# Splitting the second layer's mixer weights during the first FFN up projection of a two-layer DiT block

## The chip, the cores and the metric

The kernel runs on one core of a Trainium2 chip. The metric is the time of one execution on the device in microseconds; a kernel's figure is the median of several executions.

## The reference

The reference computes two layers of a diffusion transformer block on 512 latent tokens and 256 context tokens of width 1024, all in float32. Each layer modulates the normalized tokens, sends them through four parallel mixers (gated linear attention, pooling, a spatial gating unit, a 31-wide convolution module), projects back, normalizes, and applies a convolutional FFN with a hidden width of 2816. In the last layer the context only feeds the linear attention's state.

```python
for l in range(DEPTH):                      # DEPTH = 2
    with_ctx_out = l < DEPTH - 1
    h_lat = modulate(x, m_lat[0], m_lat[1]); h_ctx = modulate(ctx, m_ctx[0], m_ctx[1])
    y_lat, y_ctx = token_mixer(h_lat, h_ctx, w_in[l], ..., with_ctx_out)
    x = layer_norm(ALPHA * x + m_lat[2] * y_lat, ...)
    f_lat = conv_ffn(modulate(x, m_lat[3], m_lat[4]), ffn_w_up[l], ffn_conv_w[l], ffn_w_down[l], ...)
    x = layer_norm(ALPHA * x + m_lat[5] * f_lat, ...)
    if with_ctx_out:
        ...                                 # the same for ctx
```

`token_mixer` multiplies the tokens by `w_in`, whose columns are the mixers' inputs; `conv_ffn` multiplies by `w_up`, convolves 3x3 over rows of 64 tokens, gates with silu and multiplies by `w_down`.

## The kernel before

Every large product is made of three matmuls, to keep float32 accuracy with operands of fewer bits. An operand is split into a high part (a copy to the type fp32r, here *hi*) and a low part (the operand minus its high part, *lo*); `mm3` accumulates hi by hi, hi by lo and lo by hi in one PSUM bank. Activations are split once a stage (tiles hl, ll for latent tokens, hc, lc for context tokens). Weights are split as they arrive: `load_w` loads a 128x1024 tile into a stage buffer `st` (three of them, `wst`), ScalarE copies it to `hi` (L147; four buffers, `whi`), and GpSimd subtracts in two halves into `lo` (L133; four buffers, `wlo`). In some places VectorE subtracts instead.

The stages follow each other in the order of the program: mixers of layer 0 (to about 265 us), output projection, FFN up projection (to about 731 us), FFN down projection (to about 938 us), then the same for layer 1, whose mixers run from about 938 to 1097 us. The stages overlap at their edges. The order on each engine's queue is set when the program is built, by the tile framework's scheduler, and every engine takes its queue in order. All loads and stores are issued from SyncE's queue (SP).

The mixers of layer 1 (`mixers(1)`, `full` false) take 18 weight tiles of `w_in`: ten feature tiles (`w_feat`, 128 columns each, first four of them in `feat_halves`, then `feat`), four of `w_tokA` (128x576) and four of `w_tokB` (128x1024) in `tok`. The token projection A needs the context columns hc, lc too, which come out of the layer norm of the last down group by way of `to_hT` (L333 to L344). From its result come the decay logits (`lg`, L546), g (L549 to L553), the cumulative sums (`cum`, L568), the decayed keys (L599), the chunk states (`kv`, L620) and the attention itself (L649 to L691). The convolution's 31 taps for two channel tiles (L703) run on VectorE in the meantime.

The first up projection (`ffn_up(0, ...)`) loops over 44 weight tiles. For each, 24 matmuls of 512 columns and 24 of 256 run on TensorE, and ScalarE and VectorE apply nine convolution taps from PSUM (L889, L891, L918); a pair of tiles is gated by ScalarE and GpSimd (L921, L922) into gT. After the load of each tile, `fill(2)` takes two units from `queue`. Before the change these are 48 units of the second layer's modulation: 32 dots on VectorE (`dot_units`, L292) and 16 row products on TensorE (`row_units`, L251). Both load into one ring of three 128x1024 buffers (tag `ms`).

Of the kernel before, what the change touches and what calls it, by code (L numbers as in the profile page):

```python
# [58 lines left out]
def kernel(  # L59
# [72 lines left out]
    def sub_lo(eng, lo, src, hi):  # L132
        eng.tensor_tensor(out=lo, in0=src, in1=f(hi), op=ALU.subtract)  # L133
# [9 lines left out]
    def load_w(src, n, lo_eng=None, st=None):  # L143
        st = st or load_st(src, n)
        hi = whi.tile([128, 1024], F32R, tag="hi", name="hi")
        lo = wlo.tile([128, 1024], F32R, tag="lo", name="lo")
        S.activation(out=hi[:, :n], in_=st[:, :n], func=AF.Copy)  # L147
        if lo_eng is V:
            sub_lo(V, lo[:, :n], st[:, :n], hi[:, :n])
        else:  # L150
            for a, b in ((0, n // 2), (n // 2, n)):
                sub_lo(G, lo[:, a:b], st[:, a:b], hi[:, a:b])
        return hi, lo

    def mm3(ps, wh, wl, xh, xl, first, last, w_stationary=True):
# [268 lines left out]
    def mixers(l, ms=None, pre=()):  # L424
# [21 lines left out]

        def feat_halves(ids):

            ws = [load_w(w_feat[l, i], D) for i in ids]
            ps = [bank(f"fl{i}") for i in ids]  # L450
            for c0, c1 in ((0, 256), (256, 512)):
                for (hi, lo), pl in zip(ws, ps):
                    for k in range(KT):
                        w = slice(k * 128, (k + 1) * 128)
                        mm3(pl[:, c0:c1], hi[:, w], lo[:, w], hl[k][:, c0:c1], ll[k][:, c0:c1], k == 0, k == KT - 1)
            return [(pl, None) for pl in ps]

        def feat(i, ctx_too):
            hi, lo = load_w(w_feat[l, i], D)
            fill(3)  # L460
            pl = bank(f"fl{i}")
            pc = bank(f"fc{i}") if ctx_too else None
            for k in range(KT):
                w = slice(k * 128, (k + 1) * 128)
                mm3(pl, hi[:, w], lo[:, w], hl[k], ll[k], k == 0, k == KT - 1)
            if ctx_too:
                for k in range(KT):
                    w = slice(k * 128, (k + 1) * 128)
                    mm3(pc[:, :CTX], hi[:, w], lo[:, w], hc[k], lc[k], k == 0, k == KT - 1)
            return pl, pc  # L470
# [3 lines left out]
            if pc is not None:  # L474
                S.activation(out=dst[:, coff:coff + CTX], in_=pc[:, :CTX], func=func, **kw)

        def tok(src, n, passes, lo_eng=None, pre=()):
            ps, ws = {}, []
            for pi, (tiles, pool) in enumerate(passes):
                for t in tiles:  # L480
                    ps[t] = bank(f"tk{t}", pool[t])
                for k2 in range(KT // 2):
                    if pi == 0:
                        ws.append(load_w(src[l, k2], 2 * n, lo_eng, pre[k2] if k2 < len(pre) else None))
                        fill(3)
                    hi, lo = ws[k2]
                    for kk in range(2):
                        k = 2 * k2 + kk
                        s = slice(kk * n, (kk + 1) * n)
                        for t in tiles:  # L490
                            xh, xl = hcol(k, t)
                            mm3(ps[t][:, :n], hi[:, s], lo[:, s], xh, xl, k == 0, k == KT - 1, False)
            return ps
# [25 lines left out]
            conv_in()  # L519


        pa = tok(w_tokA, 288, [(range(NT), {t: "big" if t < 4 else "sm" for t in range(NT)})], V if full else G, pre)
        if full:
            with tc.issue_after(behind[0]):
                nc.sync.dma_start(out=cvw, in_=convw)
# [212 lines left out]

        lat_p = (range(4), {t: "big" for t in range(4)})
        ctx_p = (range(4, 6), {t: "big" for t in range(4, 6)})  # L740
        pb = tok(w_tokB, 512, [ctx_p, lat_p] if full else [lat_p])
        r_ = mx.tile([128, NT, 256], F32, name="r")
        vg = mx.tile([128, NT, 256], F32, name="vg")
        for t0, n in spans:
# [360 lines left out]
    for l in range(DEPTH):  # L1105
# [4 lines left out]
            out_proj(l, [(0, 1), (4, 5), (2,), (3,)], {0: (2, 3), 1: (4, 5), 4: (6, 7), 5: (2, 3), 2: (4, 5), 3: (6, 7)})  # L1110
        else:
            out_proj(l, [(0, 1), (2,), (3,)], [(1, 4), (2, 3), (0, 5), (1, 4)])
        with tc.tile_pool(name=f"gT{l}", bufs=1, side="right") as gp, \
                tc.tile_pool(name=f"gs{l}", bufs=3, side="right") as gs:
            gT = [gp.tile([128, TOK if l == 0 else LAT], F32, name=f"gT{i}") for i in range(NF)]
            with ExitStack() as es:
                conv = es.enter_context(tc.tile_pool(name=f"conv{l}", bufs=2))
                if l + 1 < DEPTH:
                    ms = es.enter_context(tc.tile_pool(name="msB", bufs=3))
                    rows, dots = row_units(l + 1, 0, ms), dot_units(l + 1, ms)  # L1120
                    for i in range(8):
                        queue.extend(dots[4 * i:4 * i + 4] + rows[2 * i:2 * i + 2])
                if l == 0:
                    rings(sm=[0, 1], big=[2, 3, 4, 5, 6], md=[7])
                else:
                    rings(big=[2, 3, 0, 5, 1, 4])
                ffn_up(l, gT, conv)
            if l == 0:
                ffn_down(l, gT, gs, [(0, 1, 2, 3), (4, 5)], {0: (0, 1), 1: (2, 3), 2: (4, 5), 3: (6, 7), 4: (0, 1), 5: (2, 3)})
            else:  # L1130
                ffn_down_last(l, gT, [(0, 1), (5, 4), (6, 2), (7, 3)])
# [130 lines left out]
```

## Time and profile before

| what | us |
| --- | --- |
| median of 3 runs | 1527.33 (1527.18 to 1527.73) |
| the profiled execution | 1527.78 |
| its span, first to last instruction | 1526.0 |
| TensorE matmuls busy | 1450.8 (95%) |
| VectorE busy | 1191.2 (78%) |
| GpSimd busy | 844.5 (55%) |
| ScalarE busy | 546.3 (36%) |

The granted TensorE clock is 0.98 of 2.4 GHz in the mean. The DMA engines moved 193 MB, 126 GB/s over the span. The busy shares are means over stages that differ; a busy TensorE counts a matmul from its start to its modelled end, so the table says which engine to look at and not where time can be won. Profiles name a line of the program as L133 and a tile by its name in the program; a weight split on GpSimd is `POOL lo L133`, its copy on ScalarE `ACT hi L147`.

### The profile page before, as it was taken

The page shows a single profiled execution, that of the slowest core. Times are in us where ns is not written, and L with a number is a line of the kernel's source. Part 1 is how long each engine was busy: PE and PEld are TensorE (multiplying, and loading weights), DVE is VectorE, ACT ScalarE, POOL GpSimd, SP SyncE. Part 2 cuts the span into 40 slices and gives each one's busy share as a digit, 9 for nine tenths or more (in the row PEclk, how much of TensorE's full clock was granted, in tenths as well). Part 3 has the DMA queues.
Part 4 walks back from the last instruction along what each step waited for, and adds up shares of the span by engine and source line. Part 5 has one row for each costly group of instructions (what it writes and reads, how often), then busy time and mean ns, then how long its engine had stood idle before and what let it go on. Part 6 is the DMA issues. An engine that isn't in the chain of part 4 may idle for free.

```text
span 1526.0 us, 22207 instructions
## 1 busy us (share of the span) xinstructions
PE 1450.8 (95%) x8389; PEld 1187.7 (78%) x8389; DVE 1191.2 (78%) x1896; ACT 546.3 (36%) x936; POOL 844.5 (55%) x695
## 2 busy tenths in 40 slices
PE   6999899998899999999999989989999999999997
PEld 5776567788688888888888768865678888888875
DVE  6429987796998877777432898798777999889596
ACT  5443224244223233233211235354426444443121
POOL 2433534454444444343444698646555888777374
PEclk9999899999999999999999999999999999999998
DMA  9545310635755521212433364221172323232531
GB/s 375 193 163 178 118 50 15 234 125 185 256 171 174 174 64 56 70 58 67 165 97 97 121 221 145 90 68 43 31 249 75 113 88 107 94 99 85 179 110 56
DMA packets 56827, 193.03 MB, mean 126 GB/s; under 512 B 6136, under 2 KB 6792, under 8 KB 55696
## 3 DMA queue, kind: packets, MB, share of 16 engines
q1 hardware_dynamic: 56720, 191.61, 37.4%
q8 instruction: 66, 1.08, 0.3%
q14 instruction: 41, 0.34, 0.1%
HBM read 181.08 MB, written 10.51 MB: 126 GB/s over the span
## 4 chain that ended last, share of the span: by engine, by line
PE 69%; DVE 13%; POOL 6%; DMA 5%; issue 4%; ACT 3%; SPq 0%; POOLq 0%; DVEq 0%; ACTq 0%
PE ul L157 10%; PE ul L158 10%; PE ul L159 10%; PE f L161 5%; PE f L162 5%; PE f L163 5%; POOL lo L133 3%; DVE acc L703 3%; PE uc L157 2%; PE uc L159 2%; PE uc L158 2%; PE fl L157 2%; DMA st<-in_w_up 2%; PE fl L159 1%; PE fl L158 1%
## 5 line engine op out<-in xcount | busy, mean ns | idle before, releaser
L133 POOL TENSOR_TENSOR lo<-st,hi 128x512 fp32r<-128x512 f32 (+1 forms) x336 | 469.6, 1421 | 342.9 <-ACT hi L147 298.4
L918 DVE SCALAR_TENSOR_TENSOR acc<-ul,cvw,acc 128x441 f32<-128x441 f32 (+2 forms) x660 | 437.9, 689 | 59.6 <-ACT acc L889 36.5
L147 ACT ACTIVATE hi<-st 128x1024 fp32r<-128x1024 f32 (+1 forms) x194 | 202.1, 1044 | 438.3 <-PE f L163 164.6
L158 PE MATMUL ul<-ll,hi 128*128 128x512 f32 (+1 forms) x768 | 286.1, 374 | 0.3 <-DVE ll L133 0.3
L157 PE MATMUL ul<-hl,hi 128*128 128x512 f32 (+1 forms) x768 | 284.1, 374 | 1.2 <-ACT hl L343 1.2
L159 PE MATMUL ul<-hl,lo 128*128 128x512 f32 (+1 forms) x768 | 285.0, 372 | 0.0
L161 PE MATMUL f<-hi,gh 128*128 128x512 f32 x440 | 170.9, 393 | 1.2 <-DVE gh L980 1.2
L162 PE MATMUL f<-lo,gh 128*128 128x512 f32 x440 | 172.0, 393 | 0.0
L163 PE MATMUL f<-hi,gl 128*128 128x512 f32 x440 | 163.9, 395 | 7.6 <-POOL gl L133 6.6
L157 PEld LDWEIGHTS ul<-hl,hi 128*128 128x128 f32 x768 | 143.9, 189 | 28.3 <-issue 2.5
L159 PEld LDWEIGHTS ul<-hl,lo 128*128 128x128 f32 x768 | 145.0, 189 | 25.3
L158 PEld LDWEIGHTS ul<-ll,hi 128*128 128x128 f32 x768 | 145.4, 189 | 24.8 <-DVE ll L133 0.5
L703 DVE SCALAR_TENSOR_TENSOR acc<-cy,cmw,acc 128x798 f32<-128x798 f32 (+1 forms) x120 | 129.0, 1115 | 0.8
L922 POOL TENSOR_TENSOR gT<-acc 128x768 f32<-128x768 f32 (+1 forms) x44 | 72.2, 1642 | 91.8 <-ACT acc L921 91.0
L163 PEld LDWEIGHTS f<-hi,gl 128*128 128x128 f32 x440 | 82.3, 188 | 28.5 <-POOL gl L133 9.3
L157 PE MATMUL uc<-hc,hi 128*128 128x256 f32 x352 | 100.5, 286 | 0.0
L889 ACT ACTIVATE acc<-ul,cvw 128x512 f32<-128x512 f32 x88 | 59.9, 681 | 113.4 <-PE ul L159 101.8
L158 PE MATMUL uc<-lc,hi 128*128 128x256 f32 x352 | 100.5, 285 | 0.0
L159 PE MATMUL uc<-hc,lo 128*128 128x256 f32 x352 | 100.3, 285 | 0.0
L161 PEld LDWEIGHTS f<-hi,gh 128*128 128x128 f32 x440 | 82.8, 188 | 20.7 <-issue 1.8
L162 PEld LDWEIGHTS f<-lo,gh 128*128 128x128 f32 x440 | 82.8, 188 | 18.0
L980 DVE CAST gh<-gT 128x256 fp32r<-128x256 f32 x66 | 39.0, 595 | 64.9 <-PE f L162 64.9
(302 smaller groups left out, 2790.9 us busy)
## 6 DMA issues: line engine op xcount, KB each, us to landing
st<-in_w_up SPq DMA_DIRECT2D x88, 512.0 KB, 3.5
st<-in_w_down SPq DMA_DIRECT2D x66, 512.0 KB, 3.6
ms<-in_wmodR SPq DMA_DIRECT2D x48, 512.0 KB, 3.3
ms<-in_wmodT SPq DMA_DIRECT2D x32, 512.0 KB, 3.3
st<-in_w_feat SPq DMA_DIRECT2D x20, 512.0 KB, 3.4
ms<-in_wmod SPq DMA_DIRECT2D x8, 1024.0 KB, 12.6
st<-in_w_out SPq DMA_DIRECT2D x16, 512.0 KB, 3.5
x<-z SPq DMA_DIRECT2D x16, 512.0 KB, 2.7
```

The lines of the kernel that those rows point to most:

```text
L133: eng.tensor_tensor(out=lo, in0=src, in1=f(hi), op=ALU.subtract)
L147: S.activation(out=hi[:, :n], in_=st[:, :n], func=AF.Copy)
L157: PE.matmul(ps, wh, xh, start=first, stop=False)
L158: PE.matmul(ps, wh, xl, start=False, stop=False)
L159: PE.matmul(ps, wl, xh, start=False, stop=last)
L161: PE.matmul(ps, xh, wh, start=first, stop=False)
L162: PE.matmul(ps, xh, wl, start=False, stop=False)
L163: PE.matmul(ps, xl, wh, start=False, stop=last)
L703: V.scalar_tensor_tensor(out=acc[i][:, :cw], in0=src, scalar=wj, in1=acc[i][:, :cw], op0=ALU.mult, op1=ALU.add)
L889: S.activation(out=a[:, :LAT], in_=pl, func=AF.Copy, scale=cw[:, 4:5])
L918: V.scalar_tensor_tensor(out=d, in0=u, scalar=w, in1=d, op0=ALU.mult, op1=ALU.add)
L922: G.tensor_tensor(out=gT[i][:, :n], in0=ag[:, :n], in1=aa[:, :n], op=ALU.mult)
```

## The change

The 18 weight tiles of `w_in[1]` are split during the first up projection. `split_units` makes 18 units. A unit loads a tile into an `ms` buffer, copies the high part into a tile `sh` (one buffer), subtracts in place in the `ms` buffer on GpSimd, and stores both parts to DRAM. They stand in `queue` in pairs, ahead of the last dot of each group of four; the last group has four. `load_split` then loads both parts straight into a `hi` and a `lo` buffer in the mixers of layer 1. The pool `gs`, with the split halves of gT for the down projection, is opened after the up projection's pools have closed instead of before they open.

```diff
+    split = {}
+
+    def split_units(srcs, ms):
+
+        def step(key, src, n):
+            st = ms.tile([128, 1024], F32, tag="ms", name="ms")
+            hi = ms.tile([128, 1024], F32R, tag="sh", name="sh", bufs=1)
+            d = [dram.tile([128, n], F32, name=f"w{p}_{key[0]}{key[1]}") for p in "hl"]
+            nc.sync.dma_start(out=st[:, :n], in_=src)
+            S.activation(out=hi[:, :n], in_=st[:, :n], func=AF.Copy)
+            lo = st.bitcast(F32R)
+            for a, b in ((0, n // 2), (n // 2, n)):
+                sub_lo(G, lo[:, a:b], st[:, a:b], hi[:, a:b])
+            nc.sync.dma_start(out=d[0], in_=f(hi[:, :n]))
+            nc.sync.dma_start(out=d[1], in_=st[:, :n])
+            split[key] = d
+
+        return [lambda x=x: step(*x) for x in srcs]
+
+    def load_split(key, n):
+        hi = whi.tile([128, 1024], F32R, tag="hi", name="hi")
+        lo = wlo.tile([128, 1024], F32R, tag="lo", name="lo")
+        for t, d in zip((hi, lo), split[key]):
+            nc.sync.dma_start(out=f(t[:, :n]), in_=d)
         return hi, lo
...
-            ws = [load_w(w_feat[l, i], D) for i in ids]
+            ws = [load_split(("f", i), D) for i in ids]
...
-            hi, lo = load_w(w_feat[l, i], D)
+            hi, lo = load_w(w_feat[l, i], D) if full else load_split(("f", i), D)
...
-                        ws.append(load_w(src[l, k2], 2 * n, lo_eng, pre[k2] if k2 < len(pre) else None))
+                        ws.append(load_w(src[l, k2], 2 * n, lo_eng, pre[k2] if k2 < len(pre) else None) if full
+                                  else load_split((name, k2), 2 * n))
...
-        with tc.tile_pool(name=f"gT{l}", bufs=1, side="right") as gp, \
-                tc.tile_pool(name=f"gs{l}", bufs=3, side="right") as gs:
+        with tc.tile_pool(name=f"gT{l}", bufs=1, side="right") as gp, ExitStack() as late:
...
                     rows, dots = row_units(l + 1, 0, ms), dot_units(l + 1, ms)
+                    sp = split_units([(("f", i), w_feat[l + 1, i], D) for i in range(10)]
+                                     + [(("a", k), w_tokA[l + 1, k], 576) for k in range(4)]
+                                     + [(("b", k), w_tokB[l + 1, k], 1024) for k in range(4)], ms)
                     for i in range(8):
                         queue.extend(dots[4 * i:4 * i + 4] + rows[2 * i:2 * i + 2])
+                        for _ in range(2 if i < 7 else 4):
+                            queue.insert(len(queue) - 3, sp.pop(0))
...
             if l == 0:
+                gs = late.enter_context(tc.tile_pool(name=f"gs{l}", bufs=3, side="right"))
                 ffn_down(l, gT, gs, [(0, 1, 2, 3), (4, 5)], {0: (0, 1), 1: (2, 3), 2: (4, 5), 3: (6, 7), 4: (0, 1), 5: (2, 3)})
```

## Rows read from the trace of the kernel before

**Rows 1.** Windows: stretch; busy us (instructions) of each engine; granted clock; DMA share; GB/s.
```profile
351.00:411.00 60.00, 52.23 (x358) 45.46 (x358) 48.63 (x82) 18.89 (x33) 24.66 (x18) 0.92 0.69 241
411.00:640.00 229.00, 229.00 (x1372) 199.56 (x1371) 195.01 (x329) 68.26 (x98) 103.22 (x70) 1.00 0.38 124
...
850.00:938.00 88.00, 77.87 (x363) 60.97 (x362) 82.31 (x124) 38.83 (x55) 78.77 (x72) 1.00 0.55 177
...
938.00:1097.00 159.00, 144.28 (x1028) 115.10 (x1026) 133.57 (x206) 67.88 (x151) 92.15 (x71) 0.95 0.21 67
```

**Rows 2.** Waits of TensorE, 938 to 1100 us: us in total, times, longest.
```profile
PE kv L620 <- DVE g L599: 6.7, 3, 4.2
PE cum L568 <- DVE g L553: 2.9, 1, 2.9
PE tk L161 <- DVE ht L339: 2.3, 1, 2.3
```

**Rows 3.** Chain of waits, 925 to 1000 us: start, us, what.
```profile
957.85 0.68 ACT hi L147
...
958.60 1.73 POOL lo L133 x2
...
989.61 1.09 ACT v L531 x4
```

**Rows 4.** Chain of waits, 1000 to 1110 us.
```profile
1007.75 0.96 DVE g L553
1008.71 16.77 DVE acc L703 x16
```

**Rows 5.** Waits of ScalarE, 938 to 1010 us.
```profile
ACT hi L147 <- DMA st<-in_w_feat: 6.7, 1, 6.7
```

**Rows 6.** Timeline of VectorE, 945 to 1060 us: start, us, what.
```profile
970.00 10.69 DVE L703 SCALAR_TENSOR_TENSOR acc<-cy,cmw,acc 128x512 f32<-128x512 f32 x16
...
984.21 16.07 DVE L703 SCALAR_TENSOR_TENSOR acc<-cy,cmw,acc 128x512 f32<-128x512 f32 x12
```

**Rows 7.** Groups by shape, 938 to 1100 us: busy us, mean ns | idle before, releasers.
```profile
L703 DVE SCALAR_TENSOR_TENSOR acc<-cy,cmw,acc 128x512 f32<-128x512 f32 x60 | 55.7, 995 | 0.0
L133 POOL TENSOR_TENSOR lo<-st,hi 128x512 fp32r<-128x512 f32 x26 | 47.4, 1848 | 32.4 <-ACT hi L147 31.6 <-POOL tmp L730 0.9
...
L133 POOL TENSOR_TENSOR lo<-st,hi 128x288 fp32r<-128x288 f32 x8 | 6.4, 825 | 2.6 <-ACT hi L147 2.6
```

**Rows 8.** DMA issues: transfers, KB each, median us from issue to landing.
```profile
ms<-in_wmodR SPq DMA_DIRECT2D x48, 512.0 KB, 3.3
...
st<-in_w_feat SPq DMA_DIRECT2D x20, 512.0 KB, 3.4
...
x<-z SPq DMA_DIRECT2D x16, 512.0 KB, 2.7
```

**Rows 9.** Groups by shape, 370 to 730 us.
```profile
L133 POOL TENSOR_TENSOR lo<-st,hi 128x512 fp32r<-128x512 f32 x82 | 112.0, 1389 | 129.6 <-ACT hi L147 128.3 <-PE mg L251 1.2
...
L147 ACT ACTIVATE hi<-st 128x1024 fp32r<-128x1024 f32 x41 | 43.5, 1061 | 84.9 <-PE uc L158 64.6 <-PE uc L159 11.0 <-PE ul L158 6.8
L922 POOL TENSOR_TENSOR gT<-acc 128x768 f32<-128x768 f32 x21 | 41.3, 1968 | 70.9 <-ACT acc L921 70.9
L292 DVE SCALAR_TENSOR_TENSOR ms<-ms,scB 128x1024 f32<-128x1024 f32 x29 | 41.2, 1422 | 8.8 <-DMA ms<-in_wmodT 8.8
```

**Rows 10.** Tile ms: shortest, median and longest ns; first and last start.
```profile
L292 DVE SCALAR_TENSOR_TENSOR ms<-ms,scB x32: 1207/1226/2474, 364.0 to 523.9; 128x1024 f32<-128x1024 f32 x32
```

**Rows 11.** Waits of TensorE, 351 to 411 us.
```profile
PE mg L251 <- DMA ms<-in_wmodR: 6.8, 4, 3.2
```

**Rows 12.** Tile f, then the timelines of GpSimd and SP, around 731 us.
```profile
L161 PE MATMUL f<-hi,gh x440: 387/392/500, 731.5 to 1514.5; 128*128 128x512 f32 x147
...
738.12 1.84 POOL L922 TENSOR_TENSOR gT<-acc 128x768 f32<-128x768 f32 x1 [11.19 <-ACT acc L921]
...
739.99 0.33 SPq L397 DMA_DIRECT2D lnw<-in_post_w  x1
```

More of the change, by code (lines that the diff above doesn't have):

```diff
@@ L152, in load_w @@
                 sub_lo(G, lo[:, a:b], st[:, a:b], hi[:, a:b])
+        return hi, lo
+    split = {}
[18 more added lines that the diff above has]
+            nc.sync.dma_start(out=f(t[:, :n]), in_=d)
         return hi, lo
@@ L475, in evac, with tok @@
                 S.activation(out=dst[:, coff:coff + CTX], in_=pc[:, :CTX], func=func, **kw)
-        def tok(src, n, passes, lo_eng=None, pre=()):
+        def tok(name, src, n, passes, lo_eng=None, pre=()):
             ps, ws = {}, []
@@ L519, in mixers @@
             conv_in()
-        pa = tok(w_tokA, 288, [(range(NT), {t: "big" if t < 4 else "sm" for t in range(NT)})], V if full else G, pre)
+        pa = tok("a", w_tokA, 288, [(range(NT), {t: "big" if t < 4 else "sm" for t in range(NT)})], V if full else G, pre)
         if full:
@@ L740, in mixers @@
         ctx_p = (range(4, 6), {t: "big" for t in range(4, 6)})
-        pb = tok(w_tokB, 512, [ctx_p, lat_p] if full else [lat_p])
+        pb = tok("b", w_tokB, 512, [ctx_p, lat_p] if full else [lat_p])
         r_ = mx.tile([128, NT, 256], F32, name="r")
```

## The prediction

> **What bounds the kernel now.** I read the table of windows first, one window per stage, since a mean over the span mixes stages with different limits [rows 1]. TensorE sets the time: from 411 to 640 us, in the first up projection, it is busy without a gap. It loses time at three places. At the start of that projection (351 to 411 us) it is busy 52.2 of 60 us. In the last part of the first down projection (850 to 938 us) it is busy 77.9 of 88, with GpSimd at 78.8 of 88. In the second layer's mixers (938 to 1097 us) it is busy 144.3 of 159 us, so it is idle for 14.7. The clock counts as well: its mean there is 0.95 of 2.4 GHz, that is, 1.2 GHz was granted in some stretches, and 159 x 0.05 = 8.0 us of full-speed work are lost. Idle time and slow clock together are 22.7 us, the most that the second mixers can give back.
>
> The second view is TensorE's waits in that stretch [rows 2]: 6.7 us for the products g of L599, 2.9 for g of L553, 2.3 for the last rows of ht. The third is the chain of waits, to see what made those three late [rows 3, 4]. Ahead of the context columns of the token projection stand an activation that makes hi (0.68) and two GpSimd subtractions (1.73). Later ScalarE sits idle 6.7 us for a weight load [rows 5] and only then copies v, on whose neighbours in its queue the decay logits wait. Later still 16 taps of the 31-wide convolution (L703), issued ahead of L599 on VectorE's in-order queue, take 16.77 us. The fourth view, VectorE's timeline, shows that these taps can be faster: the first 16 took 10.69 us, 0.67 each; then, with GpSimd's subtractions coming through beside them, 12 took 16.07, 1.34 each [rows 6]. The 60 recorded taps took 55.7 us together [rows 7].
>
> **The change, part by part.** It removes no arithmetic. Eighteen weights of layer 1 (ten feature tiles, four of tokA, four of tokB) are split in the first up projection instead of the second mixers: 18 activations on ScalarE and 36 subtractions on GpSimd, 28 of 128x512 and 8 of 128x288.
>
> *What the mixers lose.* The subtractions of [rows 7] (47.4 + 6.4 us of GpSimd; four of the 26 stay, they are the output projection's) and the activations that feed them. First, the activation and the subtractions leave the chain ahead of the token projection: 0.68 + 1.73 = 2.4, of which TensorE shows a wait of 2.3; I take 2.3 (bounds 0 and 2.3). Second, ScalarE no longer stops for the load ahead of v. Those 6.7 us are more than the 2.9 that TensorE waits for g of L553; I take 2.9 (0 and 2.9). Third, without subtractions beside them 16 taps cost 10.69 instead of 16.77, so L599 comes 6.1 us earlier, and of the wait of 6.7 I take 6.1 (0 and 6.7). Over all 60 taps the same is 55.7 - 60 x 0.67 = 15.5 us of VectorE. Fourth, if TensorE waits less its clock should fall less often; I take half of the 8.0 us, 4.0 (0 and 8.0), because part of the slow time may lie among small matmuls that stay. The gain is 2.3 + 2.9 + 6.1 + 4.0 = 15.3 us, bounds 0 and 22.7.
>
> *What the mixers gain.* Each weight arrives as two loads straight into the hi and lo buffers, 1 MB for 0.5. A load lands 3.4 us after its issue [rows 8]; today the freed buffer is filled by an activation (1.06) and two subtractions (2 x 1.85 there), 4.8 us. So nothing is later as long as the two loads overlap; if they did not, 6.8 against 4.8 is 2 us a weight, which the three other buffers hide: in the first up projection a weight keeps TensorE (731.5 - 351) / 44 = 8.6 us for 768 columns, so 5.8 for the 512 here. The DMA share is 0.21 there [rows 1]. I take 0; if the 2 us showed at the three weights that directly follow a wait of [rows 2], it would be 6 (bounds 0 and 6).
>
> *What the up projection gains.* 18 x 1.06 = 19 us of ScalarE, 28 x 1.39 + 8 x 0.83 = 46 us of GpSimd [rows 7, 9], 18 loads and 36 stores. From 411 to 640 us ScalarE is busy 68 of 229 and GpSimd 103, so both have room, and TensorE's 229 us hide the work; without that cover it would be the 46 us of GpSimd. The loads of w_up stand behind the new transfers on SP's queue, but run three stage and four weight buffers ahead.
>
> VectorE shares that stretch. Its 32 dots (L292) read two operands from SBUF; one takes 1.21 us at best, 1.42 in the mean and 2.47 at worst [rows 9, 10]. VectorE has 229 - 195 = 34 us to spare from 411 to 640, and a mean dot at 1.6 instead of 1.42 would be 6 us, so I take 0 (bounds 0 and 10, below). The Trainium skill has a rule that speaks against the change here (SBUF, State Buffer, section Who interferes with whom): a VectorE instruction with two SBUF inputs and a GpSimd instruction that reads SBUF exclude each other, and the one that comes second is blocked for the other's whole length. The worst dot, 1.26 us over the best, agrees with that; by the rule, a dot that meets one of the added subtractions costs that much more each time, and the rival on VectorE below is this rule's outcome.
>
> The ring of three ms buffers is the real price. Units now run d d d s s d r r (dots, splits, rows), two per weight load, where it was d d d d r r: 66 units over 33 loads instead of 48 over 24. A split holds a ring buffer for load 3.3, activation 1.06, subtractions 2.8 and store 2.7, 9.9 us [rows 8, 9]; a dot holds it 3.3 + 1.42 = 4.7. TensorE already waits 6.8 us for rows units in the first 60 us [rows 11]. Two groups there now have a store (2.7) ahead of the loads of their rows, 5.4; the thinner dots (four in the first eight units, where it was six) should take half of the present wait away, 3.4. I take +2.0 (bounds -6.8 and +8).
>
> *The late gs pool.* The casts of gT, some of which could be made early, now get their buffers only when the convolution pools close. The last ms work ends around 351 + 33 x 8.6 = 635 us, long before the first down matmul at 731.5 [rows 12]. I take 0 (bounds 0 and 9.5, below).
>
> **Sum.** -15.3 + 0 + 0 + 0 + 2.0 + 0 = -13.3. The profiled execution took 1527.78 us (span 1526.0 and 1.8 around it), 0.45 above the median of the runs: 1527.78 - 13.3 = 1514.5, for the median 1514.0. Its own range is 1506 to 1521, which halves the distances to the bounds.
>
> **Rivals.**
> *Slower: ScalarE is held by the single sh buffer.* The second split of a pair may write sh only when the first one's subtractions and store are through: 2 x 1.39, and 1.97 more when a gT product stands ahead on GpSimd's queue [rows 9], 4.8 us. Behind it on ScalarE wait the activations that start the taps, and on them VectorE, the PSUM banks and TensorE. Three such pairs (14.4) eat the gain and the fourth decides: with four uncovered 1514 + 19 = 1533, with five 1538. For it: a single buffer, an in-order queue, VectorE with only 11 us to spare before 411. Against: nine pairs over 33 loads, and 34 us to spare after 411. Chance 0.14.
> *VectorE becomes the bound.* If each dot met a subtraction, 2.47 us instead of 1.42, that would be 34 us, all that VectorE has to spare; some 10 dots fall in the first 100 us, where it has least: 10 x 1.05 = 10 us, 1524. Against: GpSimd is busy under half of that stretch, and so most dots miss it. Chance 0.07.
> *The gs pool waits for all that closes with it.* The pool that opens next to it issues its first load today at 739.99, 0.03 us after the end of the last gT product [rows 12]. If gs did the same, a cast and a subtraction would put the first down matmul at about 741 instead of 731.5: +9.5, 1524. Against: gs is small and has to clear only the edge of the released space. Chance 0.05.
> *Hidden.* The moved work was beside the path: TensorE's 144 us and the chain over VectorE stay, and another wait takes the place of each, 1527 (within 0.2%, 3 us, about what a measurement of this kernel can tell from no change). Against: VectorE, at 134 of 159 us there, loses 15. Chance 0.10.
> *More than forecast.* All 22.7 and the 6.8 go: 1527.3 - 29.5 = 1498. Chance 0.08.
>
> **Numbers.** The forecast has 0.56. Faster holds it, the VectorE and gs rivals and the larger gain: 0.56 + 0.07 + 0.05 + 0.08 = 0.76; same 0.10; slower 0.14. The range 1500 to 1533 leaves out most of the larger gain and half of the slower rival.
>
> **What would show it.** Right: taps at 0.67 us in the second mixers, TensorE's waits for L553 and L599 below 2 us, a mean clock above 0.97 there, and the first up projection no longer than before within 5 us. Wrong: waits of hi on sh with TensorE gaps behind them, waits on rows units beyond 10 us, a first down matmul only after the last gT product, or new TensorE waits for the loads of split weights.

## The result: 1511.3 us, as forecast

| kernel | us, median | lowest to highest of 4 runs | ratio to before, 95% interval |
| --- | --- | --- | --- |
| before | 1527.26 | 1527.15 to 1527.73 | |
| after | 1511.3 | 1508.47 to 1513.18 | 0.9893 [0.9876, 0.9911] |

Forecast were 1514 us, a range of 1500 to 1533 and a chance of 0.76 of being faster. The medians are 15.9 us apart, the profiled executions (1527.78 and 1510.28 us, spans 1526.0 and 1508.5) 17.5, which is what the rest accounts for.

**Where the 17.5 us came from.** The stages are cut at the first matmul of a tile: ul (up projection), f (down projection), kv (chunk states), y (output projection). Before the first up projection 1.8 us went, although nothing there was edited (among the other kernels this part differs by up to 1.6 us as well); the up projection up to the first f went from 399.1 to 399.9; the first down projection took 0.5 longer; from the last f of layer 0 to y in layer 1 the time fell from 167.1 to 148.5; the rest took 1.6 longer. Sum: -1.8 + 0.8 + 0.5 - 18.6 + 1.6 = -17.5. So the mixers are the whole gain.

The windows of after, to be laid beside those of [rows 1]; the last is the second layer's mixers:

```profile
351.00:411.00 60.00, 58.15 (x386) 52.40 (x389) 48.01 (x83) 24.92 (x36) 37.38 (x27) 0.97 0.79 269
411.00:640.00 229.00, 223.73 (x1344) 192.78 (x1337) 193.41 (x316) 74.08 (x106) 128.74 (x92) 0.99 0.67 228
...
938.00:1079.00 141.00, 137.71 (x1033) 111.28 (x1032) 110.69 (x201) 57.49 (x139) 45.32 (x40) 1.00 0.34 115
```

In the mixers TensorE is idle for 141.0 - 137.71 = 3.3 us where it was 14.7, so 11.4 us of idle time are gone. The clock went from 0.95 to 1.00, and TensorE's busy time fell by 144.28 - 137.71 = 6.6 us for about the same matmuls (1028 and 1033 recorded). Together that is 18.0 us, near the 18.6 that the stage lost. The 8.0 us of the prediction were too many for the clock: of the 17.0 us at 1.2 GHz in that window of before, TensorE was busy for 12.7 only, and half of that is 6.3. GpSimd fell from 92.15 to 45.32 us, VectorE from 133.57 to 110.69. All that TensorE waits for from 938 us on, where [rows 2] had 6.7, 2.9 and 2.3:

```profile
PE y L187 <- ACT hl L865: 2.0, 1, 2.0
PE sgb L664 <- issue: 1.4, 1, 1.4
PE yaT L828 <- POOL yr L823: 0.4, 1, 0.4
```

None of the three old waits is left. Just ahead of this window, at 935.93, stands a new one, for the load of the first split weight:

```profile
PE fl L183 <- DMA hi<-wh_f: 1.1, 1, 1.1
```

The convolution's taps (L703 is now L730), as a group and in VectorE's timeline, to be laid beside [rows 6, 7]:

```profile
L730 DVE SCALAR_TENSOR_TENSOR acc<-cy,cmw,acc 128x512 f32<-128x512 f32 x60 | 42.7, 780 | 0.0
```
```profile
967.00 10.69 DVE L730 SCALAR_TENSOR_TENSOR acc<-cy,cmw,acc 128x512 f32<-128x512 f32 x16
...
979.42 8.70 DVE L730 SCALAR_TENSOR_TENSOR acc<-cy,cmw,acc 128x512 f32<-128x512 f32 x13
...
997.09 10.02 DVE L730 SCALAR_TENSOR_TENSOR acc<-cy,cmw,acc 128x512 f32<-128x512 f32 x15
```

All three blocks now run at 0.67 us a tap; in before the second had 1.34. The neighbour can be counted tap by tap. In before 31 of the 60 taps overlap an instruction of GpSimd and took 1.24 us in the mean, each from its own start to its end; the other 29 took 0.74 (back to back they follow each other at 0.67). In after only 6 have such a neighbour (1.09), and the other 54 took 0.75.

The clock, in windows of before and after; the last number but two is the share of 2.4 GHz granted. First before: from inside the wait for L599 of [rows 2] on, whose longest part is 4.2 us, 1.2 GHz was granted for ten microseconds:

```profile
1027.00:1037.00 10.00, 5.96 (x208) 4.61 (x208) 6.70 (x11) 5.84 (x16) 3.33 (x2) 0.50 0.18 54
```

After, in the corresponding stretch behind the first kv, with a wait of 1.4 us in it:

```profile
1016.00:1026.00 10.00, 8.60 (x229) 6.45 (x227) 6.76 (x9) 6.58 (x18) 3.24 (x4) 1.00 0.02 4
```

**What the up projection paid.** TensorE's waits from 351 to 731 us in after, against 6.8 us for rows units before [rows 11]:

```profile
PE uc L183 <- DVE acc L945: 6.4, 4, 4.0
PE mg L277 <- DMA ms<-in_wmodR: 0.6, 1, 0.6
```

The rows units come in time now, and as much as they gave back is lost to a new wait for VectorE, whose longest piece is 4.02 us ahead of 545.60. VectorE's timeline at that place says why:

```profile
532.77 1.38 DVE L945 SCALAR_TENSOR_TENSOR acc<-ul,cvw,acc 128x441 f32<-128x441 f32 x2
537.39 1.98 DVE L318 SCALAR_TENSOR_TENSOR ms<-ms,scB 128x1024 f32<-128x1024 f32 x1 [3.23 <-DMA ms<-in_wmodT]
...
542.79 1.28 DVE L318 SCALAR_TENSOR_TENSOR ms<-ms,scB 128x1024 f32<-128x1024 f32 x1 [0.54 <-DMA ms<-in_wmodT]
```

VectorE stands 3.23 and 0.54 us for the load of a dot (L292 is now L318) with the taps that free a PSUM bank queued behind it. Its waits of this kind from 411 to 640 us, before and after:

```profile
DVE ms L292 <- DMA ms<-in_wmodT: 8.8, 10, 2.5
```
```profile
DVE ms L318 <- DMA ms<-in_wmodT: 21.3, 14, 4.3
```

A dot finds its ring buffer later, because a split holds its own until the store of the low part has landed: from 411 to 640 us SP waits 13.1 and 8.0 us for the landing of such stores (wl_f, wl_a) before it issues a dot's load, and 5.5 of them are just ahead of the load for which VectorE stands 3.23. The stores themselves also wait at the head of SP's in-order queue, 19.8 us for sh and 14.2 for the low parts; what part of the lateness comes from that was not separated. ScalarE stands too, in its activations of tile sh:

```profile
  DMA ms<-in_w_tokA: 28.9, 4
  DMA wh_f<-sh: 16.4, 4
  DMA ms<-in_w_feat: 12.6, 6
  DMA ms<-in_w_tokB: 11.2, 2
  DMA wh_b<-sh: 7.8, 2
```

24.2 us of that are the single sh buffer being stored (wh_f, wh_b), 52.7 the raw loads. ScalarE has the room: TensorE's only long gap has its releaser on VectorE.

### The profile page after: what moved, and what is told of

Read it like the earlier page. It is cut to its first block, busy times and chain, and to the rows that moved or that the text cites. A ratio compares the mean times of both kernels' runs of the same rounds, so it can differ in the third digit from the quotient of the medians.

```text
span 1508.5 us, 22357 instructions
## 1 busy us (share of the span) xinstructions
PE 1448.1 (96%) x8389; PEld 1185.7 (79%) x8389; DVE 1172.2 (78%) x1896; ACT 544.7 (36%) x936; POOL 830.0 (55%) x695
## 4 chain that ended last, share of the span: by engine, by line
PE 62%; DVE 14%; DMA 12%; POOL 6%; issue 4%; ACT 2%; SPq 1%; POOLq 0%; DVEq 0%; ACTq 0%
PE ul L183 8%; PE ul L184 8%; PE ul L185 8%; PE f L187 5%; PE f L188 5%; PE f L189 5%; DMA ms<-in_wmodT 3%; POOL lo L133 2%; PE fl L183 2%; PE fl L185 2%; PE fl L184 2%; DVE acc L730 2%; DMA wl_f<-ms 2%; POOL ms L133 2%; PE tk L187 2%
## 5 line engine op out<-in xcount | busy, mean ns | idle before, releaser
L133 POOL TENSOR_TENSOR lo<-st,hi 128x512 fp32r<-128x512 f32 x300 | 412.2, 1397 | 228.0 <-ACT hi L147 175.1
L147 ACT ACTIVATE hi<-st 128x1024 fp32r<-128x1024 f32 (+1 forms) x176 | 184.6, 1051 | 366.1 <-PE f L189 164.1
L730 DVE SCALAR_TENSOR_TENSOR acc<-cy,cmw,acc 128x798 f32<-128x798 f32 (+1 forms) x120 | 117.0, 1016 | 0.8
L133 POOL TENSOR_TENSOR gl<-gT,gh 128x256 fp32r<-128x256 f32 x66 | 54.8, 833 | 57.8 <-DVE gh L1007 50.7
```

What stands on the lines that cost most here:

```text
L730: V.scalar_tensor_tensor(out=acc[i][:, :cw], in0=src, scalar=wj, in1=acc[i][:, :cw], op0=ALU.mult, op1=ALU.add)
```

## The experiments

The times in us between those first matmuls, read from each profile; the columns "last f..kv" and "kv..y" together are the second layer's mixers:

```
                       up: ul..f  last f..kv  kv..y  y..2nd ul  2nd ul..f   span
before                    399.1       96.6    70.5     48.6      246.5    1526.0
after                     399.9       84.8    63.7     49.1      247.6    1508.5
e1_one_split              399.5       85.8    72.0     47.8      251.6    1520.0
e2_gpsimd_back            402.6      100.5    67.7     49.1      247.7    1531.9
e3_scalar_back            398.0       83.8    67.5     49.7      246.5    1509.4
e4_idle_subs              400.5       90.9    70.2     49.1      247.1    1522.1
e5_spaced                 410.2       84.4    72.1     47.9      250.1    1528.2
e6_half_sh                401.0       84.6    63.9     49.0      246.9    1509.0
e7_splits_last            399.8       85.0    71.8     48.0      250.0    1519.1
e8_w_out_too              409.1       84.6    68.2     57.4      246.0    1530.0
e9_ahead_of_rows          406.7       85.2    71.7     47.8      250.7    1525.4
e10_one_dot_earlier       406.6       85.1    63.5     49.2      247.4    1515.1
e11_pairs_half            403.8       84.9    63.5     49.1      247.2    1512.3
e12_before_reordered      400.7       99.5    69.7     54.1      248.7    1537.0
```

**What of the moved work paid: e2, e3, e4.** The early splits stay in all three; in the mixers one half of the work is put back, or GpSimd gets subtractions whose results nobody reads.

```diff
 def load_split(key, n):                      # e2: the subtractions back
-    for t, d in zip((hi, lo), split[key]): nc.sync.dma_start(out=f(t[:, :n]), in_=d)
+    raw = {"f": w_feat, "a": w_tokA, "b": w_tokB}[key[0]][1, key[1]]
+    st = load_st(raw, n)
+    nc.sync.dma_start(out=f(hi[:, :n]), in_=split[key][0])
+    for a, b in ((0, n // 2), (n // 2, n)):
+        sub_lo(G, lo[:, a:b], st[:, a:b], hi[:, a:b])
```


> The changed kernel, but the second mixers load only the high part; the weight itself is loaded too, and GpSimd subtracts there again. Theory (GpSimd's subtractions beside VectorE's taps are what cost): taps near 0.95 us again, most of the gain lost, 1519 to 1525 us. Rival (ScalarE's activations, waiting for loads at the head of its queue, are what cost): 1514 us or less.

Measured: 1531.91 us, ratio 1.0027 [1.0016, 1.0037], 7 above the range expected. The taps and two of the old waits are back:

```profile
L733 DVE SCALAR_TENSOR_TENSOR acc<-cy,cmw,acc 128x512 f32<-128x512 f32 x60 | 57.8, 1029 | 0.0
```
```profile
PE kv L650 <- DVE g L629: 6.0, 3, 4.1
PE cum L598 <- DVE g L583: 5.3, 1, 5.3
```

It loses more than the change gave: the up projection still splits (402.6 us), and a subtraction here waits for two loads. The two shares were not separated.

```diff
 def load_split(key, n):                      # e3: the activation back
...
+    st = load_st(raw, n)
+    S.activation(out=hi[:, :n], in_=st[:, :n], func=AF.Copy)
+    nc.sync.dma_start(out=f(lo[:, :n]), in_=split[key][1])
```


> The changed kernel, but the second mixers load only the low part; the weight itself is loaded too, and ScalarE copies the high part there again. Theory (GpSimd's subtractions are what cost): taps stay near 0.7 us, most of the gain stays, 1510 to 1515 us. Rival (ScalarE's activations are what cost): 1519 us or more.

Measured: 1512.8 us, 0.9901 [0.9885, 0.9916]; taps at 781 ns. The gain is there without the activations having moved.

```diff
 def load_split(key, n):                      # e4: both loads stay, and
+    st = wst.tile([128, 1024], F32, tag="st", name="st")
+    for a, b in ((0, n // 2), (n // 2, n)):
+        sub_lo(G, st[:, a:b], f(hi[:, a:b]), hi[:, a:b])
```


> The changed kernel with 36 subtractions on GpSimd added in the second mixers: each reads a loaded high part and writes to a free buffer, and nothing waits for its result. Theory (the two engines hinder each other, whoever needs the result): taps near 0.95 us, 5 to 12 us lost, 1516 to 1523 us. Rival (only the wait of matmuls for the low parts costs): taps stay near 0.7, 1510 to 1513 us.

Measured: 1524.68 us, 0.9977 [0.9965, 0.9989], just above its range. Groups (taps, then the idle subtractions) and TensorE's two longest waits:

```profile
L733 DVE SCALAR_TENSOR_TENSOR acc<-cy,cmw,acc 128x512 f32<-128x512 f32 x60 | 53.7, 960 | 0.0
```
```profile
L133 POOL TENSOR_TENSOR st<-hi 128x512 f32<-128x512 f32 x23 | 32.8, 1451 | 34.1 <-DMA hi<-wh_b 18.2 <-DMA hi<-wh_f 15.9
```
```profile
PE kv L650 <- DVE g L629: 3.5, 3, 2.8
PE cum L598 <- DVE g L583: 2.8, 1, 2.8
```

Nobody waits for these subtractions, and the kernel loses 13.4 us against after. Of these, 6.1 stand ahead of kv (90.9 for 84.8 us in the table above). There the chain of waits runs through the taps, 13 of them just ahead of g, on which cum waits:

```profile
982.00 13.12 DVE acc L733 x13
995.12 0.60 DVE g L579
```

The 29 taps that overlap an instruction of GpSimd took 1.20 us, the other 31 took 0.74, about as in after. TensorE's waits of over 0.5 us in that part all end with VectorE (2.8, 1.1 and 0.8). So the 6.1 us are what these subtractions do to VectorE. The 6.5 us behind kv (70.2 for 63.7) are not shown to be theirs: the order of matmuls that was built there is not quite after's (0.94 of the matmuls from the first cum to y match), and e3, with the same 0.94 and no subtraction added, takes 67.5 there.

A rule of the Trainium skill (SBUF — State Buffer, section Who interferes with whom) says that a VectorE instruction with two SBUF inputs contends with a GpSimd instruction that reads SBUF; the taps at 0.96 us here against 0.78 in after agree.

**Does the up projection pay for the splits? e1, e6, e7.** e1 splits one weight, loads its two parts 18 times and leaves the other 17 weights out of the computation; e6 cuts sh into three buffers of half the width; e7 puts all splits behind all other units.

```diff
 # e1
-        for t, d in zip((hi, lo), split[key]):
+        for t, d in zip((hi, lo), split["f", 0]):
...
-                        for _ in range(2 if i < 7 else 4):
-                            queue.insert(len(queue) - 3, sp.pop(0))
+                    queue.append(sp[0])
 # e6, in split_units
-            hi = ms.tile([128, 1024], F32R, tag="sh", name="sh", bufs=1)
...
+                hi = ms.tile([128, 512], F32R, tag="sh", name="sh", bufs=3)
 # e7
-                        for _ in range(2 if i < 7 else 4):
-                            queue.insert(len(queue) - 3, sp.pop(0))
+                    queue.extend(sp)
```


> The changed kernel, but only one of the 18 weights is split in the first up projection, and the second mixers load the two parts of that one weight 18 times (17 weights are left out of the computation). Theory (the splits cost the up projection next to nothing, the whole gain is in the second mixers): those mixers as in the changed kernel, 148 us from the last first-layer down matmul to the output projection instead of 167, the up projection as in the kernel before, 1508 to 1511 us. Rival (the splits cost the up projection 5 us or more, which the gain covers): 1505 us or less.

> The changed kernel, but the high part is made in halves of 512 columns in three buffers instead of one buffer of 1024. Theory (the single buffer holds ScalarE): its waits for stores of the high part, 24 us, go, and of TensorE's 6.4 us of waits for VectorE in the up projection about a third goes. Rival (the ring of three load buffers holds ScalarE, the single buffer hardly): all of the 6.4 stays within 1 us. Total 1504 to 1516 us, with the tail's order as above.

> The changed kernel with dots and rows units in the order of the kernel before and all 18 splits behind them, from the 25th weight of the up projection on. Theory (the splits thin out the dots, which is what took the waits for rows units away, and cost nothing by themselves): the waits for rows units come back to 5 to 8 us, those for VectorE fall below 3, the up projection lasts as long as before within 2 us. Rival (splits cost wherever they stand): it lasts 4 us longer or more. Second mixers up to the chunk states as in the changed kernel; total 1506 to 1518 us.

Measured: e1 1519.68 us, 0.9945 [0.9933, 0.9956]; e6 1511.39, 0.9898 [0.9885, 0.9911]; e7 1520.9, 0.996 [0.9948, 0.9972]. The up projection takes 399.5, 401.0 and 399.8 us: splitting one weight or eighteen there makes no difference to its length as long as the splits stand as in after or behind all else, and more sh buffers give nothing. In e6 ScalarE's waits for the stores of sh halved, to 11.9 us, and TensorE's waits for VectorE fell by about a third, to 4.5 us, but waits for rows units (2.2) and modT (1.9) took their place. In e7 the waits for rows units are back (7.1 us) and those for VectorE gone (0.5), as its theory expected. In e7 TensorE has no gap from 411 to 640 us although all the splitting starts only at 535:

```profile
411.00:640.00 229.00, 229.00 (x1372) 199.53 (x1371) 188.03 (x313) 78.83 (x109) 132.49 (x98) 1.00 0.66 224
```

But e1 and e7 end above their ranges. They lose some 10 us at a place where neither was edited: kv to y takes 72.0 and 71.8 us instead of 63.7. The order of the matmuls built there differs from after's: taken row by row from the first cum to y, it is the same in e1, e5, e7 and e9, and the same in after, e6, e10 and e11, while between the two groups about 0.7 of the rows match. That gave a second theory, that the order built sets the end of the mixers.

**Where the splits stand: e5, e8, e9, e10, e11.** e8 splits the second layer's eight output weights early as well, in units behind all others; e5 spaces the splits and leaves two behind the last row products.

```diff
 # after: d d d s s d r r                 e5: d d s d d s r r, and two splits behind the last rows
-                        queue.extend(dots[4 * i:4 * i + 4] + rows[2 * i:2 * i + 2])
-                        for _ in range(2 if i < 7 else 4):
-                            queue.insert(len(queue) - 3, sp.pop(0))
+                        d = dots[4 * i:4 * i + 4]
+                        queue.extend(d[:2] + [sp.pop(0)] + d[2:] + [sp.pop(0)] + rows[2 * i:2 * i + 2])
+                    queue.extend(sp)
 # e8: as after, then
+                    queue.extend(sp)         # the eight tiles of w_out[1]
```


> The changed kernel with its units in another order: dot dot split dot dot split row row, so that no two splits stand side by side, and two splits at the end. Theory (the waits of TensorE for VectorE in the up projection, 6.4 us, come from ScalarE standing at the head of its queue before a split of a pair): these waits fall below 3 us and the up projection is 2 to 4 us shorter; the second mixers up to the chunk states as in the changed kernel. Rival (the waits come from elsewhere): 5 to 8 us of waits stay. The tail of the mixers has an order of its own in each build, which may move the time by up to 8 us either way: 1503 to 1516 us in all.

> The changed kernel with the eight tiles of the second output projection split in the up projection as well, at the end of its units. Theory (in the second output projection too, subtractions and activations for weights stand in the way): its stage, from its first matmul to the first matmul of the second up projection, 49 us now, is 3 to 6 us shorter, the first up projection as before; 1503 to 1510 us. Rival (that stage waits for the layer norm and for hl, not for weights): within 2 us of the changed kernel.

Measured: e5 1530.59 us, 1.0024 [1.0014, 1.0034]; e8 1531.42, 1.0028 [1.0017, 1.0039]. Both are far above their ranges: the first f comes at 741.0 and 741.1 instead of 730.5. In e5 TensorE's waits for VectorE are 9.4 us, where the theory had below 3. TensorE's longest wait in e8's up projection, and ScalarE's timeline there:

```profile
PE mg L293 <- ACT mr L291: 8.0, 1, 8.0
```
```profile
638.39 1.06 ACT L164 ACTIVATE sh<-ms 128x1024 fp32r<-128x1024 f32 x1 [8.65 <-DMA ms<-in_w_out]
...
641.22 0.59 ACT L291 ACTIVATE mr<-mg 128x512 f32<-128x512 f32 x1
```

ScalarE stands 8.65 us at a split whose load is late, and behind it waits mr, the copy of the row products, for which TensorE stands 8.0 (5.1 in e5). That is the slower rival's mechanism, an in-order ScalarE held at sh, with another victim than the one it named. Moreover e8 loses in the output projection (57.4 instead of 49.1 us), so splitting those weights early gained nothing; and its kv to y takes 68.2 us although 99% of its matmul order there is after's, so the order of the matmuls alone does not settle that time. The next two separate the two theories; the only difference between them is the place of the splits by one dot.

```diff
 # e9: as e5, but all splits ahead of the last rows (d d s d d s r r, last group d d s d d s s s r r)
+                        queue.extend(d[:2] + [sp.pop(0)] + d[2:] + [sp.pop(0)] + (sp if i == 7 else []) + rows[2 * i:2 * i + 2])
 # e10: d s d d s d r r
+                        queue.extend(d[:1] + [sp.pop(0)] + d[1:3] + [sp.pop(0)] + (sp if i == 7 else []) + d[3:] + rows[2 * i:2 * i + 2])
```


> Units run d d s d d s r r, and the last two splits stand ahead of the last two row products instead of behind them; all else as in e5_spaced. Theory (ScalarE: a split whose load is late stood ahead of the activation mr behind the last row product, and TensorE waited 5 to 8 us for mr): with no split behind the last rows that wait goes, the first down matmul comes back from 741.0 to 730 to 733 us. The built order of the mixers' end is the one of e1, e5 and e7, so that part keeps their 72 us from the first chunk state to the output projection (after: 63.7): 1519 to 1523 in all. Rival (the spaced order itself costs the up projection, by the ring): the first down matmul stays near 740, 1530.

> As e9_ahead_of_rows, but each split stands one dot earlier (d s d d s d r r). Built so, the mixers' end has the same order of matmuls as after. Theory (the order built for the mixers' end sets it): 63 to 65 us from the first chunk state to the output projection where e9 has 72, up projection as e9, 1509 to 1514 in all. Rival (where the splits stand in the up projection moves the end of the mixers by itself): as e9, 1519 to 1523.

Measured: e9 1525.9 us, 0.9989 [0.9975, 1.0002]; e10 1518.04, 0.994 [0.9924, 0.9956]. Of the first theory a third holds: in e9 the wait for mr is gone, but the first f comes back only from 741.0 to 737.2, still 6.7 later than in after. TensorE's waits from 351 to 742 us are 11.6 us there and 7.0 in after, 9.2 of them for VectorE, as in after at 545.60. So spacing the splits costs the up projection by itself, which was the rival's point. That it does so by the ring is not shown: VectorE's waits for the loads of dots are 22.3 us from 411 to 640 in e9 and 21.3 in after. The second theory holds for the part it was about: with equal up projections (406.7 and 406.6) kv to y takes 71.7 us in e9 and 63.5 in e10. Both totals lie above their ranges, since neither has after's up projection. TensorE's timeline at that end, e9:

```profile
1080.47 0.67 PE L713 MATMUL o<-v,g 64*64 64x64 f32 x8
...
1084.57 0.84 PE L805 MATMUL cT<-cst,yn 128*128 128x128 f32 x4
1088.71 1.11 PE L828 MATMUL yaT<-cst,yr 128*128 128x128 f32 x4 [3.29 <-POOL yr L823]
1094.97 0.80 PE L187 MATMUL y<-hi,hl 128*128 128x512 f32 x1 [5.15 <-ACT hl L865]
```

and e10:

```profile
1076.44 0.67 PE L713 MATMUL o<-v,g 64*64 64x64 f32 x8
...
1083.01 0.43 PE L842 MATMUL s<-mw,vg 128*64 128x128 f32 x2
1083.86 0.66 PE L828 MATMUL yaT<-cst,yr 128*128 128x128 f32 x4 [0.42 <-POOL yr L823]
1086.56 0.50 PE L187 MATMUL y<-hi,hl 128*128 128x512 f32 x1 [2.05 <-ACT hl L865]
```

The same work ends in waits of 8.4 us in one order and 2.5 in the other. The 8.2 us between the two builds stand in three places. The last attention products (o, L713) give, by way of VectorE and GpSimd, the rows yr. In e9 they start at 1080.47, 57.2 us behind the first kv, and in e10 at 1076.44, 53.4 us behind it: 3.8 us. In e9 8.2 us pass until yaT, but the matmuls behind them last only to 1085.4; in e10 7.4 us pass, and the matmuls behind them last to 1083.4. So e9's order leaves 2 us less of other matmuls to cover that chain, and the chain itself is 0.8 us longer: GpSimd's power for rsg takes 2.05 us there, 1.64 in e10, and stands behind another one, in e9's timeline of GpSimd

```profile
1082.45 0.94 POOL L194 TENSOR_TENSOR rs_cm<-rs_cm,nhalf 128x2 f32<-128x2 f32 x1 [7.22 <-DVE rs_cm L193]
1083.36 2.05 POOL L194 TENSOR_TENSOR rsg<-rsg,nhalf 128x8 f32<-128x8 f32 x1
```

The third piece is from yaT to y, 6.3 us in e9 and 2.7 in e10: 3.6 us. y waits for hl, the high part of kT, which ScalarE copies from yaT. In e9 the copies of three weights of the output projection (wh) stand ahead of hl in ScalarE's queue:

```profile
1090.29 0.46 ACT L831 ACTIVATE kT<-yaT,half 128x256 f32<-128x256 f32 x1
...
1091.45 2.95 ACT L882 ACTIVATE wh<-st 128x1024 fp32r<-128x1024 f32 x3
1094.29 0.62 ACT L865 ACTIVATE hl<-kT 128x512 fp32r<-128x512 f32 x1
```

In e10 they do not:

```profile
1084.55 0.47 ACT L831 ACTIVATE kT<-yaT,half 128x256 f32<-128x256 f32 x1 [0.73 <-PE yaT L828]
...
1085.89 0.62 ACT L865 ACTIVATE hl<-kT 128x512 fp32r<-128x512 f32 x1
```

So the order built on ScalarE counts too. Around those waits the clock was low in e9, 0.74 in the mean from 1085 to 1105 us. The second up projection is 3.3 us longer there (250.7 against 247.4); 6.8 us at 1.2 GHz lie in it, from 1159.7 on, and none in e10.

```diff
 # e11: e6's half buffers, and d d d d s s r r
+                        queue.extend(dots[4 * i:4 * i + 4] + sp[:2 if i < 7 else 4] + rows[2 * i:2 * i + 2])
+                        del sp[:2 if i < 7 else 4]
```


> The pairs of splits stand behind all four dots of a group (d d d d s s r r), and sh is three buffers of half the width. The order of the mixers' end is that of after. If ScalarE held by the one sh buffer still costs the up projection (6.4 us of TensorE waits after), this gives some of it back: 1506 to 1510. Rival (the wait is for the raw load, which the ring sets, not for sh): 1510 to 1513.

Measured: 1514.97 us, 0.9916 [0.99, 0.9932], 4 slower than after's 1511.3 and outside both expectations. VectorE's dots wait longer for their loads here than in after (21.3 us), and TensorE's longest gap, 5.4 us at 576.17, follows the longest of these waits:

```profile
DVE ms L318 <- DMA ms<-in_wmodT: 28.6, 16, 6.6
```

**Is it the order alone? e12.** The kernel before, with one dot of each group behind the rows.

```diff
-                        queue.extend(dots[4 * i:4 * i + 4] + rows[2 * i:2 * i + 2])
+                        queue.extend(dots[4 * i:4 * i + 3] + rows[2 * i:2 * i + 2] + dots[4 * i + 3:4 * i + 4])
```


> The kernel before, with one dot of each group moved behind the two row products (d d d r r d): no weight is split early. Built so, the order of matmuls in the mixers' end is close to that of after (94% of it alike, before itself 74%). Theory (the change takes away about 12 us up to the first chunk state in any order, and part of the 6.8 us behind it was the order alone): up to the first chunk state as before within 3 us, then 66 to 69 us instead of 70.5, 1522 to 1526 in all. Rival (all of the gain is the order's): 1512 to 1516.

Measured: 1535.02 us, 1.0053 [1.0038, 1.0067], above both ranges. TensorE's two longest waits in its mixers:

```profile
PE lowp L538 <- DVE lowt L530: 7.5, 1, 7.5
PE kv L620 <- DVE g L599: 4.6, 3, 3.3
```

An order of matmuls close to after's does not bring after's time while the subtractions are there: up to kv it is 99.5 us, kv to y 69.7, and the waits move. So that order of the matmuls alone is not the gain. After's order itself, on all engines, was not built with the subtractions in place; what part of the 6.8 us behind kv is the order's and what part is the vanished waits' and the clock's stays open.

## Why the prediction was right

**The three waits: 11.3 taken, 11.9 gone.** All three of [rows 2] vanished, at the size taken within 0.6 us. That the subtractions beside the taps make L599 late, and not ScalarE, is shown by e3 (activation back, gain kept) and e4 (subtractions alone back, that wait back at 3.5 us). The second term had the right size for the wrong cause: the wait for g of L553, put down to ScalarE's stop for a load, is back in e4 at 2.8 us, although ScalarE copies none of these weights there; slow taps stood ahead of g. In before, too, g of L549 starts at 1000.20, just as the 12 slow taps of [rows 6] end. The wait for ht (2.3) came back at 0.8 in e4. The taps as a group lost 55.7 - 42.7 = 13.0 us, where 15.5 were reckoned.

**The clock: 4.0 taken, 6.6 gone.** This is the mis-sized term. I kept half because some slow time might lie among small matmuls that stay; after shows 1.00 over the whole stage. The bound of 8.0 was too high, as it counted slow time in which TensorE stood idle, and with it the 22.7 us in all: 14.7 + 6.6 = 21.3. With 11.4 us of idle time and 6.6 of clock the mixers' sum is 18.0 for the 18.6 seen.

**The ring: right cause, wrong victim, +0.8 for +2.0 (the whole up projection).** I expected TensorE to keep waiting for rows units. Those waits fell from 6.8 to 0.6 us, and the ring's lateness came out at VectorE's dots instead, 6.4 us of TensorE. That the two cancel was luck of placement: four other placements of the same units among the dots (e5, e9, e10, e11) make the up projection 403.8 to 410.2 us. The working also started the projection at 351 us; its first matmul is at 332.4, so a weight keeps TensorE 9.1 us and not 8.6, which changes no term.

**Loads, GpSimd, VectorE: nothing taken, 1.1 us seen.** After has one TensorE wait for a split weight's load, 1.05 us at the first weight of the mixers, which the prediction named as a sign of being wrong; from 938 us on it has none. Such a load lands later than the 3.4 us of [rows 8], and the stores later than 2.7:

```profile
wl_f<-ms SPq DMA_DIRECT2D x10, 512.0 KB, 5.5
hi<-wh_f SPq DMA_DIRECT2D x10, 512.0 KB, 5.2
lo<-wl_f SPq DMA_DIRECT2D x10, 512.0 KB, 4.0
```

**The rivals.** ScalarE held by sh: the mechanism exists, and in e5 and e8 it stopped TensorE for 5.1 and 8.0 us; in after it cost nothing that a gap shows, and in e6 more sh buffers did not shorten the kernel (1511.39 us). VectorE bound by dots: they did lengthen, from 1.42 us [rows 9] to 1.61, 29 x 0.19 = 5.5 us from 370 to 730, but VectorE's busy time from 411 to 640 even fell (195 to 193), and more of its lateness is waiting for their loads, 21.3 - 8.8 = 12.5. The late gs pool: the first f came at 730.5, so no. Hidden: the stage lost 18.6 us and the kernel 15.9, so no; of the three waits none was replaced by one of its size.

**What the prediction did not have.** It read the mixers as one stage whose order stays. The runs show two parts: up to kv 10.8 to 12.8 us are gained in all ten kernels without these subtractions in the mixers, whatever the order; behind kv after gains 6.8 more, and four kernels that keep the subtractions out of the mixers but have the other order (e1, e5, e7, e9) lose 1.2 to 1.6 there. With that order this change would be worth about 7 us (e1, e7) instead of 16. That it was built with the better one was luck: no term of the sum has it, and at 1520 us the forecast of 1514 would have been 6 too low. Its own narrow range (1506 to 1521) halves, on the slow side, only the distance to no gain at all; with the ring's bound of +8 it would have ended near 1525. Why a moved unit in the first layer makes the scheduler build one or the other was not tried, nor was e7's gapless up projection with after's order, which could beat after.

## What to carry to other kernels

Work taken off GpSimd paid here through the VectorE instructions that ran beside it: cost it at those instructions, with and without the neighbour, before counting any wait for its result. To learn which engine makes a result late, put back the work without its result, as e4 does. When units in a shared ring are moved, ask for each engine which of its units now finds its buffer late, and what stands behind that unit in its queue. Before a variant is judged, compare the built order, on every engine, of the stages that it does not touch; between e9 and e10 the end of the mixers alone differs by 8 us, half of what was to be measured.

## What was not expected of the hardware

Two gaps of TensorE of about the same length cost very different stretches of clock. In before the wait of 4.2 us ahead of the small matmuls of kv came with 10.2 us at 1.2 GHz, from 1026.7 on, and in them TensorE waited for another 2.5. In after the gap of 4.02 us ahead of 545.60 was followed by 3.4 us at 1.2 GHz, in which TensorE was busy throughout:

```profile
546.20:549.60 3.40, 3.40 (x18) 3.40 (x18) 2.47 (x5) 0.00 (x0) 0.00 (x0) 0.50 0.58 210
```

The length of a gap alone did not tell how much clock it would cost.

Transfers of 512 KB on SP's queue landed later in after. From 351 to 640 us the rows loads took 5.5 us instead of 3.2, and the new stores 5.0 and 5.5, at a DMA share of 0.69 instead of 0.44 in that window. In the mixers the loads of split weights of w_feat took 5.2 (hi) and 4.0 (lo), where a weight took 3.4, at a share of 0.34 instead of 0.21. Whether the share is the cause was not tested.
